# S5 parameters ahead of the input tiles, input weights split one tile ahead, and output matrices built for eight groups at a time

## The chip, the cores and the metric

The kernel runs on one core of one Trainium2 chip. The metric is the device time of one execution in microseconds (us). An engine is named by what it does: TensorE (PE: matmul, PEld: its weight load), VectorE (DVE), ScalarE (ACT), GpSimd (POOL) and SyncE (SP), whose queue issues nearly all transfers.

## What is computed

One layer of a hybrid diffusion backbone on 128 context tokens and 512 latent tokens (640 in all, 1024 channels): a token mixer with an S5 state-space branch and a pooling branch, and a squared-ReLU MLP, each with a modulated layer norm before and a gated residual after it. Cut to the part around the change:

```python
def s5_direction(u, s0, lam_re, lam_im, log_dt, b_re, b_im, c_re, c_im, d, reverse):
    dt = exp(log_dt)                       # 64 groups of 16 channels, 64 states each
    lam_bar = exp(lam * dt)
    b_bar = ((lam_bar - 1.0) / lam) * b_mat
    bu = einsum('blgh,gph->blgp', u, b_bar)
    _, s = associative_scan(a = lam_bar, bu, reverse)   # s[t] = lam_bar * s[t-1] + bu[t]
    return einsum('blgp,ghp->blgh', s, c_mat).real + d * u, s[last]

def token_mixer(h, s0_f, s0_b, grid_w, lp):
    z = h @ w_in + b_in                    # 3584 columns: u_a 1024, u_b 512, g_a 1024, g_b 1024
    y_f, y_b = s5_direction(u_a, ...), s5_direction(u_a, ..., reverse=True)
    v = gelu(y_f + y_b)
    v = v * sigmoid(v @ w_glu + b_glu)
    yb = pool_mix(u_b) @ w_proj_b
    return (sigmoid(g_a) * (v @ w_proj_a) + sigmoid(g_b) * yb) @ w_out + b_out
```

## The kernel before

All matrices are float32. A matmul with full precision is made of three passes over two halves (high, low) of both operands, so each weight tile is loaded (`wr`), its high half cast on ScalarE (L321) and its low half subtracted on VectorE (L322) by `wsplit`. One tile of the input projection (128 output channels, 640 tokens) is 48 matmuls of 320 columns at L336: eight steps over the input channels, three passes, two halves of the tokens. There are 28 such tiles: 0 to 7 give u of the S5 branch, 8 to 11 the pooling input, 12 to 27 the gates. `wr` has two buffers, `wh`, the split tile, three.

The S5 branch works on blocks of eight tokens. The 640 tokens are 80 blocks, and within a block the recurrence is done by matrices, between blocks by a scan of 63 steps of the state (`scan_step`, four VectorE operations each, L501 to L504; the first steps after step 0 do both sequences at once). The matrices are made in the kernel:

- `s5_angles` and `s5_params` (L104 to L210) turn `lam` and the time steps into powers of lam_bar: tables `pqt`, `pqs` for the output and `pwt`, `pws` for the input matrices. They are chains of short operations on VectorE with one Sin and a few copies on ScalarE.
- `gen_in(e)`, for four groups each and e from 0 to 15, makes the input matrix `wt`: it loads coefficients, forms a sum and a difference on GpSimd (L438, L439, in `coefs`), and calls `outer`, five VectorE operations of 512 elements (L424 to L431). Eight transposes on TensorE (L466) and copies on ScalarE give `w`. `in_proj(e)` then multiplies it by u, 32 small matmuls on `psz` (L480), and ScalarE writes the result into the states `zt` (L485). u comes back through DRAM in another layout, forward (`ud`) and with the blocks reversed by GpSimd (`urd`, L369, L370).
- `gen_q(e)` makes the output matrix `q` of four groups in the same way from `cpk`, and writes it to DRAM (`qd`). `gen_t(m)` multiplies the q of eight groups with the input matrices kept in `bm`, 64 small matmuls on `psq` (L533), and evacuates the result as `sq` by ScalarE (L538, L539) and VectorE (L540, L542). `psq` takes one of the two double PSUM banks that the tiles of the input projection take as well.

In program order: layer norm of the five token tiles `xs`; the first modulation; a loop over eight channel tiles that makes the normalised input `hx` and at once the input tiles 0 and 1, with `s5_angles` in the middle; `s5_params` after it; then a loop over tiles 2 to 7 with two `more_in` steps (each a `gen_in` and, one behind, an `in_proj`) after each tile, and `gen` (two `gen_q` and a `gen_t`) after tiles 5 and 7; five more `more_in`; then the scan with a `gen` in every ninth step, six in all, and one further input tile (`fill`, through `plain`) in every third step, sixteen in all. The last four tiles are computed in halves (`halves`, L606) among the steps of `out_proj`, after the scan.

Program order isn't the order on the engines. When the kernel is built, a planner walks through the program and queues, on each engine, the operation that comes first in the program among those whose inputs and buffers it expects to be ready. At run time each engine then works through its queue in order, and waits where an input is late. The number of buffers of a tile (`bufs`) thus also decides how early an operation can be queued. `q5` (the q of four groups) and `sq` have two buffers, `c3` (their coefficients) three, `b3` (coefficients of the input matrices) and `oy` (a scratch tile of `outer`) two and one.

Of the kernel before, what the change touches and what calls it, by code (L numbers as in the profile page):

```python
# [10 lines left out]
F32 = mybir.dt.float32  # L11
# [27 lines left out]
def hybrid_kernel(ctx: ExitStack, tc: tile.TileContext, xin, cc, w_ada0, w_ada, w_in, w_glu, w_pa, w_pool, w_pb,  # L39
# [263 lines left out]

    xs = []
# [4 lines left out]
    dma(lamt, lam)  # L309
# [45 lines left out]
    qd = dp.tile([16, P, 8 * P], F32, name="qd")  # L355
# [16 lines left out]

    hx = []
    hl0, hl1 = wsplit(w_in[0]), wsplit(w_in[1])
    wss += [shift_scale_load(q) for q in (1, 2, 3)]
    shift_scale(0)
    pu0, pu1 = bank2(), bank2()
    for k in range(KT):
# [11 lines left out]
        if k == 4:  # L390
            ang = s5_angles()
# [8 lines left out]
    s5_params(*ang)  # L400
# [13 lines left out]
    oyt = sub_tile("oy", 1, genp)  # L414

    def outer(o, tab, tsum, cf, e, sign):


        sh = [P, 4, TC, 16]
        tr, ti, ts = [t[:, 4 * e:4 * e + 4, :].unsqueeze(3).broadcast_to(sh) for t in (tab[:, 0], tab[:, 1], tsum)]  # L420
        c0, c1, c2 = [cf[:, :, f, :].unsqueeze(2).broadcast_to(sh) for f in (1, 3, 4)]
        o0, o1 = [o[:, :, r, :].rearrange("p l (s i) -> p l s i", i=16) for r in range(2)]
        y = oyt(sh, "oy")
# [8 lines left out]

    def coefs(tile_of, src, e, sign):

        c = tile_of([P, 4, 5, 16], "cf")
        dma(c[:, :, 1:3, :], src[:, e])
        E = nc.gpsimd
        E.tensor_tensor(c[:, :, 3, :], c[:, :, 1, :], c[:, :, 2, :], op=ALU.add)  # L438
        E.tensor_tensor(c[:, :, 4, :], c[:, :, 2 if sign > 0 else 1, :], c[:, :, 1 if sign > 0 else 2, :],  # L439
                        op=ALU.subtract)  # L440
        return c
# [13 lines left out]
    def gen_in(e):  # L455

        b3 = coefs(sub_tile("b3", 2), bpk, e, 1)
        wt = mat4([P, 4, 2, P], "wt")
        outer(wt, pwt, pws, b3, e, 1)
# [48 lines left out]
    c3t, qgt, sqt = sub_tile("c3", 3, genp), sub_tile("q5", 2, genp), sub_tile("sq", 2, genp)  # L508

    def gen_q(e):  # L510

        c3 = coefs(c3t, cpk, e, -1)
        S.mul(c3[:, :, 0, :], c3[:, :, 2, :], -1.0)
        q = qgt([P, 4, 2, 160], "q")
        S.copy(q[:, :, :, 0:16], c3[:, :, 1::-1, :])
        S.copy(q[:, :, :, 144:160], c3[:, :, 1::-1, :])
        outer(q[:, :, :, 16:144], pqt, pqs, c3, e, -1)
        dma(qd[e].rearrange("p (l r c) -> p l r c", l=4, r=2), q[:, :, :, 16:144])
        qs[e] = q

    def gen_t(m):
# [3 lines left out]
        for gq in range(2):  # L525
            e = 2 * m + gq
            q = qs.pop(e)
# [57 lines left out]
    def plain(m, func, dst):  # L585
        ps = mm(wsplit(w_in[m]), hx)
        g = gt([P, NT], "g")
        S.activation(tv(g), v2(ps), func, bias=colt[:, C_BIN + m:C_BIN + m + 1])
        dma(dst, g)
# [606 lines left out]
```

## Time and profile before

| | us |
|---|---|
| median of 3 runs | 1055.24 |
| lowest and highest run | 1054.97, 1055.71 |
| the profiled execution, its own time | 1057.73 |
| its span, first to last instruction | 1056.0 |

| engine | busy us | share of the span |
|---|---|---|
| TensorE matmul | 991.3 | 94% |
| TensorE weight load | 894.4 | 85% |
| VectorE | 691.6 | 65% |
| ScalarE | 403.0 | 38% |
| GpSimd | 110.9 | 11% |

The profile is one execution; times in it are counted from the start of its span. Matmuls are pipelined and their ends are modelled, so a stretch in which TensorE counts as busy can still hold less work than it could. A row of the timeline merges instructions of a kind that follow each other; its length is from the start of the first to the end of the last, and operations that follow each other overlap a little, so a spacing is read from start to start. What stands in brackets is the idle time of the engine before the row, and what ended it.

### The profile page before, as it was taken

To read this page: it belongs to the slowest core of one execution; us is meant where nothing else is said; L and a number is where in the kernel's file an instruction comes from. 1 tells how busy PE (TensorE), PEld (TensorE's weight loads), DVE (VectorE), ACT (ScalarE), POOL (GpSimd) and SP (SyncE) were. 2 spreads that over 40 slices of the span, in tenths; PEclk is the share of its full clock that TensorE was granted. 3 is DMA by queue.
4 is the path that set the end of the run, shared out by engine and by line. 5 is a ranking of instruction groups with operands and counts; after the bars stand their busy time and mean duration, and the time that the engine had idled before them with its cause. 6 is when DMAs were issued, how large, how long until landed. Compare 5 with 4: busy or idle time off the path is not lost.

```text
span 1056.0 us, 18416 instructions
## 1 busy us (share of the span) xinstructions
PE 991.3 (94%) x7464; PEld 894.4 (85%) x7464; DVE 691.6 (65%) x1203; ACT 403.0 (38%) x683; POOL 110.9 (11%) x164
## 2 busy tenths in 40 slices
PE   4998989998998899999999999989999999999997
PEld 2887878988897799998987898868998899889886
DVE  7698769998921334545847955498864586458686
ACT  5457454322212534422222544313661266116610
POOL 0243210310069000300000000000000000000000
PEclk9999899999999798999999999999999999999999
DMA  9566666855498587977752134513222222212421
GB/s 362 191 176 179 168 182 194 255 166 170 119 284 248 161 253 244 360 231 252 247 182 83 31 110 155 150 45 100 81 100 73 68 80 100 80 60 81 162 78 60
DMA packets 117373, 166.85 MB, mean 158 GB/s; under 512 B 48104, under 2 KB 80872, under 8 KB 117288
## 3 DMA queue, kind: packets, MB, share of 16 engines
q1 hardware_dynamic: 111912, 146.27, 43.9%
q0 software_dynamic: 5376, 19.40, 5.4%
q8 instruction: 59, 0.97, 0.4%
q14 instruction: 26, 0.21, 0.1%
HBM read 135.30 MB, written 30.34 MB: 157 GB/s over the span
## 4 chain that ended last, share of the span: by engine, by line
PE 61%; DVE 16%; DMA 10%; issue 6%; ACT 5%; SPq 2%; DVEq 0%; ACTq 0%; POOL 0%; POOLq 0%
PE ps L336 20%; PE ps L1073 13%; PE ps L1006 8%; PE psx L1006 6%; PE pse L1096 3%; PE ps L886 3%; DVE wh L322 2%; DMA cf<-in_cpk_dram 2%; DMA yd<-y 2%; DVE ta L501 1%; DVE zt L504 1%; PE psa L236 1%; PE psz L480 1%; DVE ta L503 1%; PE ps L1096 1%
## 5 line engine op out<-in xcount | busy, mean ns | idle before, releaser
L336 PE MATMUL ps<-hk,wh 128*128 128x320 f32 x1344 | 217.1, 318 | 10.0 <-DVE sq L542 5.1
L336 PEld LDWEIGHTS ps<-hk,wh 128*128 128x128 f32 x1344 | 202.0, 192 | 18.6 <-issue 6.0
L322 DVE TENSOR_TENSOR wh<-wr,wh 128x1024 fp32r<-128x1024 f32 (+1 forms) x113 | 128.5, 1138 | 101.8 <-ACT wh L321 100.7
L321 ACT CAST wh<-wr 128x1024 fp32r<-128x1024 f32 (+1 forms) x113 | 109.3, 967 | 164.7 <-PE ps L1073 87.6
L1073 PE MATMUL ps<-wh,fx 128*128 128x512 f32 x720 | 166.1, 392 | 5.2 <-DVE x L852 3.0
L1073 PEld LDWEIGHTS ps<-wh,fx 128*128 128x128 f32 x720 | 135.7, 189 | 34.2 <-DVE x L852 3.4
L336 PEld LDWEIGHTS ps<-gx,wh 128*128 128x128 f32 x384 | 56.4, 187 | 3.3 <-issue 2.9
L336 PE MATMUL ps<-gx,wh 128*128 128x320 f32 x384 | 58.7, 310 | 0.0
L336 PEld LDWEIGHTS ps<-vx,wh 128*128 128x128 f32 x384 | 56.4, 188 | 2.5 <-ACT sg L813 2.1
L336 PE MATMUL ps<-vx,wh 128*128 128x320 f32 x384 | 58.1, 311 | 0.0
L224 POOL DMA_DIRECT2D wa<-in_w_ada_dram x32 | 16.9, 534 | 300.8 <-PE psa L236 110.2
L1006 PE MATMUL psx<-h,wh 128*128 128x320 f32 x288 | 47.5, 308 | 0.0
L1006 PE MATMUL ps<-h,w 128*128 128x320 f32 x288 | 46.5, 307 | 0.0
L438 POOL TENSOR_TENSOR cf<-cf 128x64 f32<-128x64 f32 x32 | 24.8, 776 | 191.0 <-DMA cf<-in_cpk_dram 95.7
L1006 PEld LDWEIGHTS psx<-h,wh 128*128 128x128 f32 x288 | 43.7, 187 | 0.2
L1006 PEld LDWEIGHTS ps<-h,w 128*128 128x128 f32 x288 | 43.2, 187 | 0.0
L573 PE MATMUL psy<-zt,q 64*128 64x80 f32 x512 | 42.1, 276 | 0.6 <-issue 0.6
L851 DVE TENSOR_TENSOR ps<-ps,gate 128x512 f32<-128x512 f32 (+2 forms) x39 | 28.1, 749 | 19.2 <-PE ps L1073 14.2
L573 PEld LDWEIGHTS psy<-zt,q 64*128 64x128 f32 x512 | 35.3, 190 | 4.2 <-issue 4.2
L886 PE MATMUL ps<-wo,mx 128*128 128x512 f32 x150 | 36.6, 392 | 0.7 <-ACT wo L321 0.7
L336 PE MATMUL ps<-ybx,wh 128*128 128x320 f32 x192 | 32.6, 328 | 2.7 <-ACT wh L321 2.7
L886 PEld LDWEIGHTS ps<-wo,mx 128*128 128x128 f32 x150 | 27.9, 188 | 7.2 <-ACT wo L321 1.5
(263 smaller groups left out, 1656.9 us busy)
## 6 DMA issues: line engine op xcount, KB each, us to landing
wr<-in_w_m_dram SPq DMA_DIRECT2D x64, 512.0 KB
wa<-in_w_ada_dram POOLq DMA_DIRECT2D x32, 512.0 KB, 5.0
wr<-in_w_in_dram SPq DMA_DIRECT2D x28, 512.0 KB
qd<-q SPq DMA_DIRECT2D x16, 512.0 KB
q<-qd SPq DMA_DIRECT2D x16, 512.0 KB
x<-in_xin_dram SPq DMA_DIRECT2D x10, 512.0 KB
wa<-in_w_ada_dram SPq DMA_DIRECT2D x10, 512.0 KB
tm<-sd SPq DMA_DIRECT2D x8, 512.0 KB
```

The source lines that it names most:

```text
L224: nc.gpsimd.dma_start(w, w_ada[self.mod, :, k * D:(k + 1) * D])
L236: T.matmul(self.ps[32 * q:32 * q + 32, 0:256], sc[:, k, :], w[:, q * 256:(q + 1) * 256], start=(k == 0), stop=(k == KT - 1), skip_group_ch ...
L321: S.copy(hi, raw)
L322: V.tensor_tensor(lo, raw, hi.bitcast(F32), op=ALU.subtract)
L336: T.matmul(ps[:, n, 0:ln], hl[:, wh, k * P:(k + 1) * P], xk[:, xh, o:o + ln], start=(k == 0 and i == 0), stop=(k == nk - 1 and i == 2))
L438: E.tensor_tensor(c[:, :, 3, :], c[:, :, 1, :], c[:, :, 2, :], op=ALU.add)
L573: T.matmul(o, q[d, l, i, :], zt[d, 0:NC // 2, i, 4 * e + l, :], start=(i == 0), stop=False, skip_group_check=True)
L851: V.tensor_tensor(ps, ps, g[:, c0:c1], op=ALU.mult)
L886: T.matmul(ps[:, n, :], mx[k][:, xh, t * P:(t + 1) * P], wo[k][:, wh, n * 512:(n + 1) * 512], start=(k == 0 and i == 0), stop=(k == KT - 1 ...
L1006: T.matmul(ps, hl[:, wh, c + k * P:c + (k + 1) * P], rq[b][:, xh, k, :], start=(start and k == 0 and i == 0), stop=(stop and k == 3 and i ...
L1073: T.matmul(pt[t], fx[k][:, xh, t * P:(t + 1) * P], hl[:, wh, kk * 512:(kk + 1) * 512], start=(k == 0 and i == 0), stop=(k == 7 and i == 2))
L1096: T.matmul(ps[n][:, 0:ln], fx[k][:, xh, t * P:(t + 1) * P], hl[:, wh, o_:o_ + ln], start=(k == 0 and i == 0), stop=(k == 7 and i == 2))
```

## The change

`lam` is loaded ahead of the five token tiles. `s5_angles` and `s5_params` are called one after the other ahead of the loop over the channel tiles. `next_w` hands out the split weights of the input tiles in the order in which they are used and splits one more than is asked for. `gen_q` makes q for eight groups in operations of 1024 elements; `q5` and `sq` have one buffer, `c3` two, `b3` three. Coefficients are formed in place: three columns where there were five. `gen_q(0)` stands ahead of the loop over tiles 2 to 7, and each further `gen_q` behind the `gen_t` of the eight groups before; `gen_t(0)` and `gen_t(1)` come after tiles 4 and 6, `gen_t(2)` and `gen_q(3)` before the last three `more_in`. One `fill` stands before the scan; in the scan are five `gen_t` and four `gen_q`, eleven steps apart, and fifteen `fill`, in every fourth step. The work of the input projection, of `gen_in` and of the output stage is the same; the scratch of q in DRAM has rows twice as long.

```diff
@@ -301,12 +301,12 @@
             V.scalar_tensor_tensor(modc[:, mod, 2 * q:2 * q + 2, :], src[:, mod, :, 0:2], float(mod), b,
                                    op0=ALU.add, op1=ALU.add)
+    dma(lamt, lam)
     xs = []
     for t in range(NTT):
         x = mat4([P, D], "x")
         xs.append(x)
         dma(x, xin[t])
-    dma(lamt, lam)
     dma(ident, cst)
     dma(colt, cols)
     wss = [shift_scale_load(0)]
@@ -352,7 +352,7 @@
     urd = dp.tile([KT, TC, P, NC], F32, name="urd")
     yd = dp.tile([KT, TC, P // 8, 8 * NC], F32, name="yd")
     sd = dp.tile([KT, 32, 4, 480], F32, name="sd")
-    qd = dp.tile([16, P, 8 * P], F32, name="qd")
+    qd = dp.tile([KT, P, 16 * P], F32, name="qd")
     mbd = dp.tile([KT, P, NT], F32, name="mbd")
     gad = dp.tile([KT, P, NT], F32, name="gad")
     gbd = dp.tile([KT, P, NT], F32, name="gbd")
@@ -370,10 +370,19 @@
         nc.gpsimd.tensor_copy(ur[:, :, CP:NC], uj[:, :, NC - 1:CP - 1:-1])
         dma(urd[m].rearrange("j p c -> p j c"), ur)
+    order_w, ready_w = [*range(2, 12), *range(20, 28), *range(12, 20)], []
+    def next_w():
+        while order_w and len(ready_w) < 2:
+            ready_w.append(wsplit(w_in[order_w.pop(0)]))
+        return ready_w.pop(0)
     hx = []
     hl0, hl1 = wsplit(w_in[0]), wsplit(w_in[1])
     wss += [shift_scale_load(q) for q in (1, 2, 3)]
     shift_scale(0)
+    s5_params(*s5_angles())
     pu0, pu1 = bank2(), bank2()
     for k in range(KT):
         pa, pb = bank("pst"), bank("pst")
@@ -387,8 +396,6 @@
         V.tensor_copy(hk[:, 0, :], hf)
         V.tensor_tensor(hk[:, 1, :], hf, hk[:, 0, :].bitcast(F32), op=ALU.subtract)
         hx.append(hk)
-        if k == 4:
-            ang = s5_angles()
         if k % 2:
             if k < KT - 1:
                 shift_scale(k // 2 + 1)
@@ -397,7 +404,6 @@
                     mm_k(pu, hl, hx[kk], kk, KT, SEG)
     ua_evac(0, pu0)
     ua_evac(1, pu1)
-    s5_params(*ang)
     dma(dd, ddg)
     V.tensor_tensor(dd[:, 0, :], dd[:, 0, :], dd[:, 1, :], op=ALU.add)
@@ -411,16 +417,17 @@
     dma(s0t, s0)
-    oyt = sub_tile("oy", 1, genp)
-    def outer(o, tab, tsum, cf, e, sign):
-        sh = [P, 4, TC, 16]
-        tr, ti, ts = [t[:, 4 * e:4 * e + 4, :].unsqueeze(3).broadcast_to(sh) for t in (tab[:, 0], tab[:, 1], tsum)]
-        c0, c1, c2 = [cf[:, :, f, :].unsqueeze(2).broadcast_to(sh) for f in (1, 3, 4)]
+    oyt, bt = sub_tile("oy", 1, genp), sub_tile("b3", 3)
+    c3t, qgt, sqt = sub_tile("c3", 2, genp), sub_tile("q5", 1, genp), sub_tile("sq", 1, genp)
+    def outer(o, tab, tsum, cf, g0, n, sign):
+        sh = [P, n, TC, 16]
+        tr, ti, ts = [t[:, g0:g0 + n, :].unsqueeze(3).broadcast_to(sh) for t in (tab[:, 0], tab[:, 1], tsum)]
+        c0, c1, c2 = [c.unsqueeze(2).broadcast_to(sh) for c in cf]
         o0, o1 = [o[:, :, r, :].rearrange("p l (s i) -> p l s i", i=16) for r in range(2)]
-        y = oyt(sh, "oy")
+        y = oyt([P, 8, TC, 16], "oy")[:, 0:n]
         V.tensor_tensor(y, ts, c0, op=ALU.mult)
         V.tensor_tensor(o0, ti, c1, op=ALU.mult)
         V.tensor_tensor(o1, tr, c2, op=ALU.mult)
@@ -430,16 +437,6 @@
         else:
             V.tensor_tensor(o1, o1, y, op=ALU.subtract)
-    def coefs(tile_of, src, e, sign):
-        c = tile_of([P, 4, 5, 16], "cf")
-        dma(c[:, :, 1:3, :], src[:, e])
-        E = nc.gpsimd
-        E.tensor_tensor(c[:, :, 3, :], c[:, :, 1, :], c[:, :, 2, :], op=ALU.add)
-        E.tensor_tensor(c[:, :, 4, :], c[:, :, 2 if sign > 0 else 1, :], c[:, :, 1 if sign > 0 else 2, :],
-                        op=ALU.subtract)
-        return c
     bmv = bm[:, 0:G * 32].rearrange("p (g b i) -> p g b i", g=G, b=2)
     us = {}
@@ -454,9 +451,12 @@
     def gen_in(e):
-        b3 = coefs(sub_tile("b3", 2), bpk, e, 1)
+        b = bt([P, 4, 3, 16], "b")
+        dma(b[:, :, 0:2, :], bpk[:, e])
+        nc.gpsimd.tensor_tensor(b[:, :, 2, :], b[:, :, 0, :], b[:, :, 1, :], op=ALU.add)
+        nc.gpsimd.tensor_tensor(b[:, :, 1, :], b[:, :, 1, :], b[:, :, 0, :], op=ALU.subtract)
         wt = mat4([P, 4, 2, P], "wt")
-        outer(wt, pwt, pws, b3, e, 1)
+        outer(wt, pwt, pws, [b[:, :, i, :] for i in (0, 2, 1)], 4 * e, 4, 1)
         S.copy(bmv[0:64, 4 * e:4 * e + 4, :, :], wt[0:64, :, :, 0:16])
         S.copy(bmv[64:128, 4 * e:4 * e + 4, :, :], wt[64:128, :, :, P - 16:P])
         w = mat4([P, 4, 2, P], "w")
@@ -505,26 +505,27 @@
     qs, outs, tms = {}, {}, {}
-    c3t, qgt, sqt = sub_tile("c3", 3, genp), sub_tile("q5", 2, genp), sub_tile("sq", 2, genp)
-    def gen_q(e):
-        c3 = coefs(c3t, cpk, e, -1)
-        S.mul(c3[:, :, 0, :], c3[:, :, 2, :], -1.0)
-        q = qgt([P, 4, 2, 160], "q")
-        S.copy(q[:, :, :, 0:16], c3[:, :, 1::-1, :])
-        S.copy(q[:, :, :, 144:160], c3[:, :, 1::-1, :])
-        outer(q[:, :, :, 16:144], pqt, pqs, c3, e, -1)
-        dma(qd[e].rearrange("p (l r c) -> p l r c", l=4, r=2), q[:, :, :, 16:144])
-        qs[e] = q
+    def gen_q(m):
+        c = c3t([P, 8, 3, 16], "c")
+        dma(c[:, :, 0:2, :].rearrange("p (a l) r i -> p a l r i", a=2), cpk[:, 2 * m:2 * m + 2])
+        nc.gpsimd.tensor_tensor(c[:, :, 2, :], c[:, :, 0, :], c[:, :, 1, :], op=ALU.add)
+        q = qgt([P, 8, 2, 160], "q")
+        for o in (0, 144):
+            S.copy(q[:, :, 0, o:o + 16], c[:, :, 0, :])
+            S.mul(q[:, :, 1, o:o + 16], c[:, :, 1, :], -1.0)
+        nc.gpsimd.tensor_tensor(c[:, :, 1, :], c[:, :, 0, :], c[:, :, 1, :], op=ALU.subtract)
+        outer(q[:, :, :, 16:144], pqt, pqs, [c[:, :, i, :] for i in (0, 2, 1)], 8 * m, 8, -1)
+        dma(qd[m].rearrange("p (l r c) -> p l r c", l=8, r=2), q[:, :, :, 16:144])
+        qs[m] = q
     def gen_t(m):
         ps2 = bank2("psq")
         pss = [ps2[:, 0], ps2[:, 1]]
         for gq in range(2):
-            e = 2 * m + gq
-            q = qs.pop(e)
+            e, q = 2 * m + gq, qs[m][:, 4 * gq:4 * gq + 4]
             for r in range(2):
                 c0 = 4 * e * 32 + r * 16
                 for fb in range(2):
@@ -551,7 +552,7 @@
             dma(tm.rearrange("p l a f -> p (l a) f"), src)
             tms[m] = tm
         q = qt([P, 4, 2, P], "q")
-        dma(q.rearrange("p l r c -> p (l r c)"), qd[e])
+        dma(q.rearrange("p l r c -> p (l r c)"), qd[m][:, (e % 2) * 1024:(e % 2) * 1024 + 1024])
         u = ut([P, 4, NC], "u")
         for hf, d in enumerate((ud, urd)):
             dma(u[64 * hf:64 * hf + 64], d[m, 4 * hf:4 * hf + 4].rearrange("j (i g) c -> (j i) g c", g=8)
@@ -583,7 +584,7 @@
     def plain(m, func, dst):
-        ps = mm(wsplit(w_in[m]), hx)
+        ps = mm(next_w(), hx)
         g = gt([P, NT], "g")
         S.activation(tv(g), v2(ps), func, bias=colt[:, C_BIN + m:C_BIN + m + 1])
         dma(dst, g)
@@ -596,7 +597,7 @@
         while fillers:
             m, func, dst = fillers.pop(0)
-            hl, ps = wsplit(w_in[m]), bank2()
+            hl, ps = next_w(), bank2()
             for k in range(KT):
                 mm_k(ps, hl, hx[k], k, KT, SEG)
                 if k == 3:
@@ -624,17 +625,18 @@
     nin = [0]
-    def gen(m):
-        gen_q(2 * m)
-        gen_q(2 * m + 1)
-        gen_t(m)
+    gen_q(0)
     for m in range(2, 8):
-        ua_evac(m, mm(wsplit(w_in[m]), hx))
+        ua_evac(m, mm(next_w(), hx))
         more_in(2, 1)
-        if m in (5, 7):
-            gen((m - 5) // 2)
-    more_in(5)
+        if m in (4, 6):
+            gen_t(m // 2 - 2)
+            gen_q(m // 2 - 1)
+    more_in(2)
+    fill(1)
+    gen_t(2)
+    gen_q(3)
+    more_in(3)
     prectx.close()
     sub[0] = s5ctx.enter_context(tc.tile_pool(name="post", bufs=1, reuse_waits="tile"))
     qt, tmt = sub_tile("q", 4), sub_tile("tm", 3)
@@ -708,9 +710,11 @@
             S.copy(last, state(CP))
             dma(nstate, last)
             S.copy(state(CP), s0t)
-        if s % 9 == 5 and s // 9 < 6:
-            gen(2 + s // 9)
-        if s % 3 == 0 and s < 48:
+        if s % 11 == 3 and s < 50:
+            gen_t(3 + s // 11)
+            if s < 40:
+                gen_q(4 + s // 11)
+        if s % 4 == 0 and s < 60:
             fill(1)
     genctx.close()
     mixctx = ctx.enter_context(ExitStack())
```

## Rows read from the trace of the kernel before

**Rows 1.** stretches: start:end, length; PE, PEld, DVE, ACT, POOL busy; clock, DMA, GB/s

```profile
0.00:52.60 52.60, 36.11 (x396) 29.18 (x396) 35.19 (x123) 25.97 (x47) 6.30 (x18) 1.00 0.75 277
67.10:92.00 24.90, 21.31 (x232) 18.47 (x233) 22.37 (x32) 18.04 (x43) 8.92 (x14) 1.00 0.74 199
103.10:113.60 10.50, 7.00 (x71) 5.03 (x72) 8.72 (x13) 3.15 (x9) 1.68 (x4) 0.67 0.85 224
135.90:144.80 8.90, 5.61 (x75) 4.28 (x74) 8.56 (x13) 2.78 (x9) 0.76 (x2) 0.81 0.79 220
158.00:166.00 8.00, 5.43 (x73) 4.71 (x73) 6.91 (x11) 5.73 (x17) 1.92 (x4) 0.79 0.19 50
52.60:170.00 117.40, 104.37 (x1120) 92.62 (x1120) 92.28 (x147) 69.15 (x171) 33.34 (x59) 0.94 0.63 168
170.00:291.00 121.00, 112.64 (x1092) 108.80 (x1091) 112.35 (x318) 33.78 (x70) 14.17 (x16) 1.00 0.63 190
```

**Rows 2.** groups of TensorE's matmuls, 52.6 to 170 us: busy, mean ns, idle before

```profile
L336 PE MATMUL ps<-hk,wh 128*128 128x320 f32 x352 | 60.6, 323 | 0.0
L480 PE MATMUL psz<-u,w 128*64 128x80 f32 x512 | 28.3, 254 | 0.0
L466 PE MATMUL pst<-ident,wt 128*128 128x128 f32 x128 | 19.7, 286 | 6.2 <-DVE wt L427 6.2
L533 PE MATMUL psq<-q,bm 64*32 64x128 f32 x128 | 3.6, 310 | 6.8 <-DVE q L427 6.8
```

**Rows 3.** the same groups in the scan stage, 170 to 291 us

```profile
L336 PE MATMUL ps<-hk,wh 128*128 128x320 f32 x707 | 106.7, 310 | 7.8 <-DVE sq L542 5.1 <-ACT g L588 2.7
L533 PE MATMUL psq<-q,bm 64*32 64x128 f32 x384 | 6.9, 274 | 0.0
```

**Rows 4.** timeline of TensorE around the first matrix step: start, length, operation, idle before

```profile
99.75 1.03 PE L466 MATMUL pst<-ident,wt 128*128 128x128 f32 x8
100.72 1.33 PE L480 MATMUL psz<-u,w 128*64 128x80 f32 x32
101.97 1.09 PE L466 MATMUL pst<-ident,wt 128*128 128x128 f32 x8
106.60 0.66 PE L533 MATMUL psq<-q,bm 64*32 64x128 f32 x16 [3.53 <-DVE q L427]
```

**Rows 5.** timeline of SyncE's queue, ScalarE and VectorE: the S5 parameters and their surroundings

```profile
3.56 0.49 SPq L309 DMA_DIRECT2D big<-in_lam_dram  x1
...
29.04 0.27 ACT L295 COPY row<-psa 128x128 f32<-128x128 f32 x1 [5.87 <-PE psa L292]
...
65.02 0.89 DVE L209 TENSOR_TENSOR pws<-pwt 128x512 f32<-128x512 f32 x1 [0.37 <-ACT pwt L208]
```

**Rows 6.** timeline of VectorE: the split of the input tile before that step

```profile
103.51 1.23 DVE L322 TENSOR_TENSOR wh<-wr,wh 128x1024 fp32r<-128x1024 f32 x1 [2.91 <-ACT wh L321]
```

**Rows 7.** timeline of VectorE, then its group of L431 from 170 to 291 us

```profile
126.18 0.68 DVE L426 TENSOR_TENSOR wt<-pwt,cf 128x512 f32<-128x512 f32 x1
126.78 0.68 DVE L427 TENSOR_TENSOR wt<-oy,wt 128x512 f32<-128x512 f32 x1
...
272.61 1.22 DVE L322 TENSOR_TENSOR wh<-wr,wh 128x1024 fp32r<-128x1024 f32 x1
273.75 0.28 DVE L503 TENSOR_TENSOR ta<-ta,zt 128x128 f32<-128x128 f32 x1
...
L431 DVE TENSOR_TENSOR q<-q,oy 128x512 f32<-128x512 f32 x10 | 6.9, 691 | 0.0
```

**Rows 8.** waits from 170 to 291 us: total, times, longest

```profile
ACT cf L513 <- DMA cf<-in_cpk_dram: 44.7, 5, 15.2
...
POOL ub L654 <- PE psq L533: 26.7, 1, 26.7
```

**Rows 9.** timeline of GpSimd: the same copy twice

```profile
60.81 4.00 POOL L369 COPY ujr<-uj 128x128 f32<-128x128 f32 x1 [5.46 <-ACT uj L364]
...
133.74 0.29 POOL L369 COPY ujr<-uj 128x128 f32<-128x128 f32 x1 [3.30 <-ACT uj L364]
```

## The prediction

> **What bounds the kernel now.** I read the busy times of the engines stretch by stretch first, because one average over the span (TensorE 94% busy) hides four stages with different limits [rows 1]. Up to 52.6 us the layer norm, the first modulation and the first two input tiles run; from 52.6 to 170 the input projection of the S5 branch with the generation of its matrices; from 170 to 291 the serial scan on VectorE with sixteen gate tiles ("fillers") on TensorE beside it; from 291 to 412 the output projection. What follows is nearly solid matmul and isn't touched. A busy TensorE isn't a working one, so next I priced its work in the two middle stages by its groups [rows 2, 3]. In the scan 707 matmuls of 320 columns take 106.7 us, 0.151 each, and 64 of the small matmuls on psq take 6.9 / 6 = 1.15. From the timeline eight transposes take 0.97 (99.75 to 100.72) and 32 matmuls of the state input 1.25 (100.72 to 101.97) [rows 4]. By these prices the second stage holds 352 x 0.151 + 512 x 0.039 + 128 x 0.121 + 2 x 1.15 = 91.0 us of work in 117.4 us: 26.4 are lost. The scan stage holds 106.7 + 6.9 = 113.6 in 121: 7.4 lost, beside a VectorE busy 112.35; both engines are near their limit there. So the second stage is the place.
>
> Then the waits say where the 26.4 lie. The matrix step L533 waits 6.8 us in two pieces for q and the transposes L466 wait 6.2 for wt, both VectorE's outer products [rows 2]. Around the first L533, 103.1 to 113.6, the 71 matmuls (by the timeline 32 on psq, 7 on ps, 32 on psz: 2.9 us by the prices; the kinds of the next stretches are counted in the same way) take 10.5: 7.6 lost, more than the wait of 3.53 itself, because the granted clock of that stretch is 0.67, that is, it fell to the 1.2 GHz level after the idle time [rows 1, 4]. Around the second, 135.9 to 144.8, 8.9 us hold 3.1: 5.8 lost, clock 0.81. From 158 to 166, 8.0 hold 3.5: 4.5 lost. From 67.1 to 92, where the S5 matrices have only just begun, 24.9 hold 57 x 0.151 + 48 x 0.121 + 128 x 0.039 = 19.4: 5.5 lost. These four are 23.4 of the 26.4; 3.0 are scattered.
>
> **Part A, S5 parameters first (to 52.6 us).** The load of lam goes ahead of five x loads on SyncE's queue. Its issue is 0.49 [rows 5], so each x, and the first layer norm, starts up to 0.49 later. What it serves: today the last of the parameters on VectorE, the sum L209, starts at 65.02 and ends at 65.9, and no wt can be built before that [rows 5]. Moved up, at most 65.9 - 52.6 = 13.3 us of VectorE work go ahead of 52.6, with q of the first eight groups (5.7, below). VectorE is busy 35.19 of these 52.6, so 17.4 are free [rows 1]: 13.3 + 5.7 - 17.4 = 1.6 don't fit. I take 1.6 + 0.49 = +2.1. Lower end +0.5, the issue alone, if the other work slides behind 52.6 without harm. Upper end: all 13.3 are queued ahead of the first hk and cover only the 5.87 us in which ScalarE waits for the modulation matmuls [rows 5]: +7.4. The steps on ScalarE (a Sin with its table load, eight copies) lie in the same gap; if the Sin falls between two square roots, two more table loads come, and I leave them to this end too.
>
> **Part B, the second stage.** Its work afterwards: 6 x 48 matmuls for u, one filler of 48, the same 512 and 128, and three psq steps: 336 x 0.151 + 20.0 + 15.5 + 3.45 = 89.7. The losses, one by one. (1) The two stalls on q, 13.4: gen_q now stands one step ahead of the gen_t that reads it (q of groups 0 to 7 before the loop, the next right behind each gen_t), and the weight tile of the next input matmul is split one tile ahead, so TensorE has both at hand. I take them at 0; upper end 13.4. Both are needed: at 103 us TensorE had no split weight either, since the cast on ScalarE came last (L322 at 103.51, 2.91 us idle on VectorE) [rows 6]. (2) The start, 5.5: the wt of the first groups no longer wait for L209; the u that come back through DRAM still are as late as now, so I take 2.5. (3) The tail, 4.5: VectorE waits behind coefficient loads; fewer and larger ones now, 3.0. (4) The scattered 3.0 stay. (5) New waits. VectorE gets four double q here (22.8 us, below) for six single ones; the trace can't show how the new order meshes, and I put 5.0 there: four waits of the size of a transposing wait, 6.2 / 5 [rows 2]. Lost: 13.5, so 103.2 us against 117.4: -14.2. Ends: the loss rate of the scan stage (7.4 in 121) would leave 89.7 + 5.9 = 95.6, -21.8; the old 26.4 would leave 116.1, -1.3.
>
> The double operations: one outer product is five operations of 512 elements at a spacing of 0.60 (126.18 to 126.78), 3.0 us; one of 1024 elements spaces 1.14 (272.61 to 273.75), so five are 5.7 for two, 0.3 saved a pair, 2.4 in all [rows 7]. Half the issues of q and of its coefficients also leave SyncE's queue; nothing on the path waits for those issues alone, so 0 for that.
>
> **Part C, the scan.** TensorE: 15 fillers and five gen_t, 720 x 0.151 + 5 x 1.15 = 114.5. VectorE: ten outer products go (one operation of each is the row of L431, x10), 30.0, and four double ones come, 22.8: 112.35 - 7.2 = 105.2 [rows 1, 7]. So TensorE bounds it, plus its waits: 7.8 now, 5.1 for the last step of sq (psq shares two PSUM pairs with the fillers) and 2.7 for g on ScalarE [rows 3]. The latter stands behind L513, which waits 44.7 us in five pieces for coefficients [rows 8]; with two slots for one load in each period they can come a period early: 0. Of the 5.1 I keep 4.0. 118.5 against 121: -2.5. Ends: no wait -6.5, the old waits +1.3.
>
> At the same place a rule speaks against longer operations. The row first: GpSimd's copy L369 of 128 elements takes 0.29 alone, and 4.00 while VectorE runs without a pause, six of its operations long [rows 9]. The Trainium skill, "SBUF — State Buffer", section "Who interferes with whom", says that a VectorE operation with two SBUF inputs and a GpSimd operation that reads SBUF take the port as an exclusive lock for a whole instruction. By it an operation of 1.14 in place of 0.60 holds a u copy 0.54 longer, and if all eight copies were on the path the sum would be 4 us higher; by the row GpSimd waits for a pause, not for the end of one operation, and the length costs 0. That row decides for the sum.
>
> **Part D, the output stage.** Unchanged work; q is read from rows twice as long in DRAM, in pieces of the same size: 0. GpSimd's pooling there starts only once the last psq is done (a wait of 26.7 [rows 8]); the last gen_t moves from step 50 to 47 of the scan, which may start it some steps earlier: lower end -5, upper end +3 if its reads of SBUF fall into the scan.
>
> **Sum.** The profiled execution took 1057.73 us (span 1056.0), 2.49 above the median of 1055.24. 1057.73 + 2.1 - 14.2 - 2.5 = 1043.1; less 2.49, **1041** for the median.
>
> **Rivals.** First, **the waits only change their name**: VectorE's outer products and the way of u through DRAM pace the second stage whatever the order. For it: wt is a wait already [rows 2], and VectorE is busy 92.28 of 117.4 there [rows 1]. Against: TensorE stalls at the same moments as VectorE, on work that could have been done before. Half of B left gives 1048; the low end of B gives 1055.24 + 2.1 - 1.3 - 2.5 = 1054. Second, **slower: the single q buffer**. It was two tiles of four groups, now it is one of eight, so gen_q(m+1) can't write before the 64 matmuls of gen_t(m) are done and q has been written to DRAM. VectorE runs in order: behind the waiting operation stand the scan steps and the splits, and behind these TensorE. A gen_t can stand behind one filler, 48 x 0.151 = 7.2, so the wait is up to 7.2 + 1.15 = 8.4 for each of seven gen_q; half of it, seven times, is +29: 1070. It decides from (1057.4 - 1041) / 7 = 2.3 us each. Against: operations are queued by when the planner expects their inputs, and VectorE's waits in the scan are small today [rows 3, 6]. Third, **more than forecast**: B at the loss rate of the scan, 1041 - 7.6 = 1033, and with pooling earlier 1028.
>
> **How the numbers follow.** Forecast, 1034 to 1048: 0.48. Better, 1026 to 1034: 0.13. Between 1048 and 1053.1: 0.10. Within 0.2% (1053.1 to 1057.4, what a measurement can tell from no change): 0.10. Slower, by the q buffer or the upper end of A with no gain in B: 0.19. Faster is 0.71. The range leaves out some 0.05 below 1027 and 0.15 above 1058.
>
> **What would show it.** Right: no idle time of L533 for q, the granted clock at 1.00 between 100 and 145, the first wt before 60 us, the scan's first steps near 158, and a scan stage of about 118. Wrong: an L425 or L424 on VectorE waiting for psq or for q's write (the second rival); L466 or L480 waiting longer than now (the first); the loop over the channel tiles ending several us after 52.6 (A's upper end).

## The result, and the profile after

The changed kernel takes **1065.28 us** (median of 4 runs, 1062.74 to 1067.66), where the kernel before takes 1055.47 (4 runs): a ratio of 1.0088, interval 1.0059 to 1.0117. It is 0.9% slower, and outside the forecast's range. Its profiled execution has a span of 1062.9 us, 6.9 more than before.

First the stretches of the changed kernel, in the columns of [rows 1]: two that stand in [rows 1] as well, and then the four stages at their own bounds.

```profile
0.00:52.60 52.60, 31.79 (x372) 26.72 (x372) 44.97 (x141) 28.97 (x49) 7.74 (x20) 1.00 0.76 273
52.60:170.00 117.40, 110.32 (x1304) 99.91 (x1304) 86.59 (x116) 65.41 (x166) 30.73 (x49) 0.99 0.70 196
...
0.00:60.10 60.10, 37.61 (x399) 32.12 (x399) 51.08 (x150) 30.52 (x52) 7.94 (x20) 0.97 0.76 266
60.10:171.60 111.50, 104.56 (x1279) 94.53 (x1278) 81.60 (x108) 65.45 (x166) 30.53 (x48) 1.00 0.70 194
171.60:278.80 107.20, 104.59 (x928) 102.08 (x928) 102.68 (x270) 29.70 (x55) 22.13 (x20) 1.00 0.67 200
278.80:300.70 21.90, 0.03 (x1) 0.02 (x1) 21.59 (x23) 1.84 (x2) 21.53 (x23) 0.55 0.27 85
```

Up to 52.6 us VectorE has 45.0 us of work instead of 35.2 and TensorE falls behind (31.8 instead of 36.1). In the second stage TensorE does 184 more instructions in the same 117.4 us (128 of them the small ones on psq), at a clock of 0.99 instead of 0.94. And there is a stretch that before didn't have: 21.9 us in which TensorE does nothing, while VectorE and GpSimd are both busy throughout, with 23 instructions each. The timeline of TensorE shows the bounds of the stages:

```profile
60.14 3.05 PE L336 MATMUL ps<-hk,wh 128*128 128x320 f32 x19
...
142.10 0.53 PE L480 MATMUL psz<-u,w 128*64 128x80 f32 x4 [2.34 <-DMA u<-ud]
...
171.57 10.67 PE L336 MATMUL ps<-hk,wh 128*128 128x320 f32 x71 [1.55 <-ACT g L589]
...
300.71 1.15 PE L574 MATMUL psy<-zt,q 64*128 64x80 f32 x8 [21.88 <-POOL us L667]
```

TensorE's timeline of the kernel before, at the same points:

```profile
176.13 21.39 PE L336 MATMUL ps<-hk,wh 128*128 128x320 f32 x144
...
289.28 1.16 PE L533 MATMUL psq<-q,bm 64*32 64x128 f32 x64
291.00 0.68 PE L573 MATMUL psy<-zt,q 64*128 64x80 f32 x8 [0.56 <-issue]
```

The channel-tile loop ends at 60.14, where tile 2 begins (before: 52.6). At 171.57 there are 672 matmuls of input tiles left ahead of the output stage; the kernel before comes to that point at 176.13, with one matrix step fewer done. The output stage begins at 300.71 (before: 291.00). So the 6.9 us are made of these four:

| stage, us | before | after | difference |
|---|---|---|---|
| to the end of the channel-tile loop | 52.6 | 60.1 | +7.5 |
| to 672 matmuls left | 123.5 | 111.4 | -12.1 |
| to the first matmul of the output stage | 114.9 | 129.1 | +14.3 |
| the rest | 765.0 | 762.2 | -2.8 |

The groups of TensorE, 52.6 to 170 us, which answer to [rows 2]; the kernel before's stall for q at L533 is gone from the group that takes its place, L534:

```profile
L336 PE MATMUL ps<-hk,wh 128*128 128x320 f32 x408 | 67.7, 320 | 2.5 <-DVE hk L396 2.0 <-DVE hk L397 0.5
L480 PE MATMUL psz<-u,w 128*64 128x80 f32 x512 | 24.6, 237 | 3.5 <-DMA u<-ud 3.5
L466 PE MATMUL pst<-ident,wt 128*128 128x128 f32 x128 | 19.1, 279 | 1.9 <-DVE wt L434 1.7
L534 PE MATMUL psq<-q,bm 64*32 64x128 f32 x256 | 6.6, 276 | 0.0
```

In the scan, 170 to 301 us, the same view shows 4.2 us of TensorE's ordinary waits (7.8 in [rows 3]):

```profile
L336 PE MATMUL ps<-hk,wh 128*128 128x320 f32 x672 | 100.6, 310 | 4.2 <-ACT g L589 2.5 <-DVE sq L543 1.7
```

What costs the time is the last piece of the third stage. GpSimd's timeline there (its spans are rough):

```profile
256.42 0.75 POOL L656 MEMSET ub<- 128x784 f32 x1 [16.20 <-PE psq L534]
...
271.22 0.55 POOL L660 DMA_DIRECT2D ic<-in_invc_dram  x1 [11.21 <-DVE ta L503]
...
273.21 1.50 POOL L667 TENSOR_TENSOR us<-ub 128x783 f32<-128x783 f32 x1
...
275.35 2.08 POOL L671 TENSOR_TENSOR ic<-us,ic 128x128 f32<-128x128 f32 x2
...
291.97 3.06 POOL L667 TENSOR_TENSOR us<-us 128x781 f32<-128x781 f32 x2
295.11 1.72 POOL L671 TENSOR_TENSOR ic<-us,ic 128x128 f32<-128x128 f32 x2
296.79 1.77 POOL L672 TENSOR_TENSOR ic<-ic,ub 128x128 f32<-128x128 f32 x2
```

and VectorE's timeline, a step of the scan just ahead of it and some rows beside it:

```profile
270.43 0.28 DVE L502 TENSOR_TENSOR tb<-lmi,zt 128x128 f32<-128x128 f32 x1
...
272.22 3.58 DVE L322 TENSOR_TENSOR wh<-wr,wh 128x1024 fp32r<-128x1024 f32 x1
...
276.20 1.37 DVE L502 TENSOR_TENSOR tb<-lmi,zt 128x128 f32<-128x128 f32 x1
...
282.89 2.00 DVE L501 TENSOR_TENSOR ta<-lmr,zt 128x128 f32<-128x128 f32 x1
...
290.81 2.82 DVE L503 TENSOR_TENSOR ta<-ta,zt 128x128 f32<-128x128 f32 x1
293.66 1.51 DVE L504 TENSOR_TENSOR zt<-ta,tb 128x128 f32<-128x128 f32 x1
...
299.03 1.57 DVE L504 TENSOR_TENSOR zt<-ta,tb 128x128 f32<-128x128 f32 x1
```

The pooling branch (`pool_mix`) begins here at 256.4, where its first memset ends a wait for the psq matmuls of the last `gen_t`, which run at 255.2 (before: at 289.3). GpSimd then waits another 11.21 us, until 271.2, before its next load; from 273.2 on its additions run while the scan is still at work. Each takes 1.5 us or a little more. An operation of the scan that takes 0.28 alone takes up to 2.82 beside them, the split at L322 3.58 instead of 1.22. From 272.22 to the end of the last L504 at 300.6 there are six scan steps and two splits. Undisturbed, a step is 1.06 from start to start and the two splits are 1.14 and 0.60, 8.1 in all; here they last 28.4. That is +20.3, and the rest of the stage gained 6.0.

### The profile page after: what moved, and what is told of

It reads as the page before. It is cut to its first block, busy times and chain, and to the rows that moved or that the text cites. A ratio compares the mean times of both kernels' runs of the same rounds, so it can differ in the third digit from the quotient of the medians.

```text
span 1062.9 us, 18300 instructions
## 1 busy us (share of the span) xinstructions
PE 986.3 (93%) x7464; PEld 894.0 (84%) x7464; DVE 706.7 (66%) x1163; ACT 400.4 (38%) x667; POOL 108.1 (10%) x148
## 4 chain that ended last, share of the span: by engine, by line
PE 60%; DVE 14%; DMA 12%; issue 6%; ACT 4%; POOL 3%; SPq 1%; DVEq 0%; ACTq 0%; POOLq 0%
PE ps L336 20%; PE ps L1077 13%; PE ps L1010 8%; PE psx L1010 6%; PE pse L1100 3%; PE ps L890 2%; PE psy L574 2%; DMA wr<-in_w_in_dram 2%; DVE wh L322 2%; DMA wa<-in_w_ada_dram 1%; PE psa L236 1%; PE psz L480 1%; DMA wr<-in_w_out_dram 1%; PE ps L1100 1%; DVE zt L504 1%
## 5 line engine op out<-in xcount | busy, mean ns | idle before, releaser
L336 PE MATMUL ps<-hk,wh 128*128 128x320 f32 x1344 | 214.6, 317 | 9.5 <-DVE hk L396 4.4
L322 DVE TENSOR_TENSOR wh<-wr,wh 128x1024 fp32r<-128x1024 f32 (+1 forms) x113 | 130.1, 1152 | 105.9 <-ACT wh L321 104.9
L574 PE MATMUL psy<-zt,q 64*128 64x80 f32 x512 | 43.9, 285 | 21.9 <-POOL us L667 21.9
L589 ACT ACTIVATE g<-ps,colt 128x640 f32<-128x640 f32 x16 | 12.7, 795 | 65.5 <-PE ps L336 65.5
```

Source lines behind the costliest of these rows:

```text
L322: V.tensor_tensor(lo, raw, hi.bitcast(F32), op=ALU.subtract)
L336: T.matmul(ps[:, n, 0:ln], hl[:, wh, k * P:(k + 1) * P], xk[:, xh, o:o + ln], start=(k == 0 and i == 0), stop=(k == nk - 1 and i == 2))
L574: T.matmul(o, q[d, l, i, :], zt[d, 0:NC // 2, i, 4 * e + l, :], start=(i == 0), stop=False, skip_group_check=True)
```

## The experiments

The kernel before had medians from 1055.5 to 1061.8 on the chips of these runs, so each kernel is compared by its ratio to the runs of the kernel before on its own chip; a difference of two medians from different chips can be off by some us.

**Pooling held until the scan is over.** In each of the four poolings one operation makes the first element of the input depend on the last state:

```diff
         E.memset(u, 0.0)
+        z = state(NC - 1)[:, 0, 0:1]
+        E.tensor_tensor(u[:, 0:1], z, z, op=ALU.subtract)
```

> The changed kernel with one edit: each pooling starts with a difference of the scan's last state, written into a column that is zero anyway, so GpSimd can't pool before the scan has ended. Theory (pooling in the scan's last steps slows VectorE: six steps and two splits take 28.8 us, 271.9 to 300.7, in place of some 8): the scan ends near 281 us, the idle time of TensorE before the output stage (21.9 us) falls under 4, and the median is 1045 to 1050. Rival (VectorE's own order delays those steps, GpSimd only fills the time): the scan still ends near 300 and the median stays at 1065 or rises, since the pooling then ends later too.

1043.7 us, ratio 0.9842 (0.9807 to 0.9877), span 1042.2: a little better than the theory said, and its rival is out. VectorE's groups from 270 to 283 us are back at their length, and TensorE's output stage begins at 280.03, in its timeline:

```profile
L322 DVE TENSOR_TENSOR wh<-wr,wh 128x1024 fp32r<-128x1024 f32 x2 | 2.4, 1222 | 1.7 <-ACT wh L321 1.7
L502 DVE TENSOR_TENSOR tb<-lmi,zt 128x128 f32<-128x128 f32 x8 | 2.3, 284 | 0.0
```

```profile
280.03 0.68 PE L574 MATMUL psy<-zt,q 64*128 64x80 f32 x8 [1.40 <-issue]
```

By the spans the hold is worth 20.7 us, by the starts of the output stage (300.71, 280.03) the same; by the ratios (0.9842 against 1.0088) it is 2.5%, some 26 us. Nothing is lost behind: from there to the end both kernels take 762.2. Pooling's later start costs nothing.

**Pooling's arithmetic left out**, its memsets and loads kept:

```diff
-            n = pool3([P, 784], "us")
...
-            E.tensor_tensor(n[:, a:b_], s[:, a - d0:b_ - d0], s[:, a + d1:b_ + d1], op=ALU.add)
+            n = s
...
-            E.tensor_tensor(iv, sv, iv, op=ALU.mult)
-            E.tensor_tensor(iv, iv, uv, op=ALU.subtract)
```

> The changed kernel with GpSimd's arithmetic of the pooling left out (its sums, products and differences; fills and loads stay). Theory: VectorE's operations from 272 us on have their old lengths (0.2 to 0.3 us for a step's operation, 1.2 for a split) and the scan ends near 280 us; 1040 to 1048. Rival: the steps stay spread out to 300 us without GpSimd's arithmetic, 1060 or more.

1044.78 us, ratio 0.9854 (0.9805 to 0.9903), as the theory said. The memsets and transfers run at the old early place, and the scan beside them is undisturbed. GpSimd's timeline, then VectorE's group of 255 to 281 us:

```profile
274.07 1.43 POOL L658 DMA_DIRECT2D ub<-ubd  x2
275.49 0.77 POOL L656 MEMSET ub<- 128x784 f32 x1
```

```profile
L502 DVE TENSOR_TENSOR tb<-lmi,zt 128x128 f32<-128x128 f32 x21 | 6.0, 284 | 0.0
```

So it is the additions and products, not pooling's memory, loads or issues.

**Pooling held on an earlier state**, four steps ahead of the last (`state(NC - 5)` in the first edit):

> The changed kernel with pooling held on the state four scan steps before the last one instead of on the last. Theory (each scan step beside pooling lasts some 3 us longer): the last four steps and what follows them stretch, TensorE's wait ahead of the output stage grows from 1.4 to 8 to 15 us, and the time is 1048 to 1057. Rival (the 20 us of the changed kernel are the cost of pooling's start, its memory or its loads, and not of each step beside it): 1042 to 1046, as when it is held on the last state.

1059.37 us, ratio 0.9998 (0.9972 to 1.0024), span 1053.5. VectorE's and TensorE's timelines:

```profile
276.12 2.00 DVE L504 TENSOR_TENSOR zt<-ta,tb 128x128 f32<-128x128 f32 x1
278.15 0.59 DVE L501 TENSOR_TENSOR ta<-lmr,zt 128x128 f32<-128x128 f32 x1
278.67 1.77 DVE L502 TENSOR_TENSOR tb<-lmi,zt 128x128 f32<-128x128 f32 x1
280.36 1.76 DVE L503 TENSOR_TENSOR ta<-ta,zt 128x128 f32<-128x128 f32 x1
282.15 1.46 DVE L504 TENSOR_TENSOR zt<-ta,tb 128x128 f32<-128x128 f32 x1
```

Scan operations that last 1 to 2 us begin with the first addition, and TensorE's wait ahead of the output stage is 12.6 us where the hold on the last state has 1.4. The time is a little above the theory's upper end; its rival is out. With six steps beside pooling the output stage begins at 300.7, with four at 291.4, with none at 280.0: the cost goes with the steps that meet it, 2.8 us each with four and 3.4 with six, or 2.9 without the 3.4 us by which the two splits among the six are longer. The trace is of the fastest of ten executions (1055.63); by the ratios (0.9998 against 0.9842) the four steps cost 1.6%, some 16 us, so 2.8 is a low figure.

**The same collision made in the kernel before.** Its matrix steps in the scan are put seven steps apart instead of nine and nothing else is changed:

```diff
-        if s % 9 == 5 and s // 9 < 6:
-            gen(2 + s // 9)
+        if s % 7 == 3 and s // 7 < 6:
+            gen(2 + s // 7)
```

> The kernel before with one edit: the output matrices of a group are made at every seventh scan step instead of every eighth plus its offset, so the last of the six is done some ten steps of the scan earlier and GpSimd's pooling may begin while the scan still runs, as it does in the changed kernel. Nothing else of the change is in it. Theory (pooling beside the scan stretches the scan's short two-input VectorE operations): pooling's first pieces stand ahead of the scan's end in the trace, the VectorE operations of the steps beside it last 1.5 to 3 us where they last 0.3 to 1.2 elsewhere, TensorE has an idle stretch of more than 10 us ahead of the output stage, and the time is 1065 to 1080 where the kernel before has 1055 to 1060. Rival (the stretch in the changed kernel comes from its larger output matrices or its split, not from pooling as such): within 3 us of the kernel before. If pooling's inputs land only after the scan's end, the run says nothing on either.

1065.01 us, ratio 1.0059 (1.0034 to 1.0085): nearly as slow as the whole change, by moving the matrix steps of the scan and nothing else. GpSimd's, VectorE's and TensorE's timelines:

```profile
284.64 1.51 POOL L665 TENSOR_TENSOR us<-ub 128x783 f32<-128x783 f32 x1
...
286.78 1.71 POOL L669 TENSOR_TENSOR ic<-us,ic 128x128 f32<-128x128 f32 x2
288.45 1.71 POOL L670 TENSOR_TENSOR ic<-ic,ub 128x128 f32<-128x128 f32 x2
```

```profile
283.68 3.03 DVE L322 TENSOR_TENSOR wh<-wr,wh 128x512 fp32r<-128x512 f32 x1
286.63 3.68 DVE L504 TENSOR_TENSOR zt<-ta,tb 128x128 f32<-128x128 f32 x1
290.35 1.46 DVE L501 TENSOR_TENSOR ta<-lmr,zt 128x128 f32<-128x128 f32 x1
```

```profile
300.10 1.14 PE L573 MATMUL psy<-zt,q 64*128 64x80 f32 x8 [9.91 <-POOL ub L654]
```

The time is at the theory's lower end and the idle stretch, 9.91, just under the 10 that it named. The mechanism needs neither the double operations nor the single q buffer nor the parameters first; it needs the last `gen_t` early. **Eight steps apart** (`s % 8 == 4`) was too mild to test it:

> The kernel before with one edit: its six matrix steps in the scan come in every eighth step in place of every ninth, the last at step 44 in place of 50, so that the memory of the matrices, on which GpSimd's pooling waits, comes free before the scan has ended. Nothing else of the change is in it. Theory (early pooling slows the scan's last steps): pooling starts 6 us or more before the scan's end, the operations of the steps beside it take 0.5 to 2 us each, and the kernel gets slower by 5 to 15 us. Rival (the slow tail belongs to the new order of the q and split operations): within 3 us of the kernel before.

1056.99 us, ratio 0.9995 (0.9971 to 1.0019). Pooling's memset came at 282.81, but GpSimd then waited 12.17 us for another transfer, until 298.6, and the first addition came at 300.6, after the scan's end; nothing met. Inconclusive.

**S5 parameters put back** (angles at the fifth channel tile, the rest behind the loop; the load of `lam` stays first), once in the changed kernel and once in the held one:

```diff
-    s5_params(*s5_angles())
...
+        if k == 4:
+            ang = s5_angles()
...
+    s5_params(*ang)
```

> The changed kernel with the two S5 calls put back (angles at the fifth channel tile, parameters behind the loop); all else as changed. Theory (S5 ahead of the channel tiles costs 7.5 us there, since VectorE is full until 58 us): the loop ends near 52 us again, the second stage starts some 7 us earlier but its input matrices come later; if these don't matter the median is 1058, and if the start of the second stage loses its old 5 us it stays within 2 us of 1065. Rival (the early parameters are what shortened the second stage): 1068 or more.

> Both edits at once: pooling held until the scan has ended, and the S5 calls put back. Theory with independent parts: the two gains add, 1038 to 1045 against 1055 of the kernel before. Rival (an earlier second stage only fills the scan with work that is late anyway): the same as the hold alone, within 2 us.

1073.04 us, ratio 1.0125 (1.007 to 1.018), and 1050.45, ratio 0.9908 (0.9876 to 0.994). The held one is 7 us slower than with the parameters first, so both its theory (1038 to 1045) and its rival (no change) were wrong. The unheld one has its rival's time (1068 or more), but its interval overlaps the changed kernel's 1.0088 (1.0059 to 1.0117). In the held one the loop ends at 51.9, 8.2 us earlier, and yet the point with 672 matmuls left comes at 176.76, 5.7 later. Its TensorE timeline shows where both are lost:

```profile
69.55 0.44 PE L468 MATMUL pst<-ident,wt 128*128 128x128 f32 x2 [2.78 <-DVE wt L436]
...
115.38 0.70 PE L482 MATMUL psz<-u,w 128*64 128x80 f32 x4 [4.73 <-DMA u<-ud]
...
176.76 5.54 PE L336 MATMUL ps<-hk,wh 128*128 128x320 f32 x36 [1.55 <-ACT g L591]
```

Neither kernel waits for q at its matrix step, though the parameters are late here, and with the parameters first alone (below) the stall stays: that leaves `gen_q`, made one step ahead and in its new form, as what removes it. This wasn't run by itself.

**Only the angles first**, the rest of the parameters behind the loop, in the held kernel:

```diff
-    s5_params(*s5_angles())
+    ang = s5_angles()
...
+    s5_params(*ang)
```

> The changed kernel with pooling held until the last state of the scan is there, and with the second half of S5's parameters put back behind the loop over channel tiles, while the angles stay ahead of it. Theory A (the 7.5 us by which the channel tiles end late are VectorE's time for the parameters, and the half that is put back needn't be early): the loop ends 3 to 5 us earlier and the time is 1038 to 1042. Theory B (the scan's first output matrix has to be ready when the filler stage begins, and the parameters are on its chain): the loop ends earlier, the stage behind it begins later, and the time is 1046 to 1052, as with both halves put back (1050).

1050.94 us, ratio 0.9918 (0.9891 to 0.9945): the loop ends at 56.2, 3.9 earlier than in the held kernel, but the 672-left point comes at 179.64 and a wait of 5.93 for u at 118.4 has come. The time is theory B's.

**S5 first alone, in the kernel before** (`lam` first, both calls ahead of the loop, nothing else):

> The kernel before with the S5 part alone: lam loaded first, angles and parameters ahead of the channel tiles. Theory after the last runs (the early parameters delay the channel tiles by some 7 us and give back more than that in the second stage): the loop ends near 58 us in place of 52.6, the second stage ends 0 to 8 us earlier than before, 1047 to 1056 against 1055 (where the scan ends before pooling starts). Rival (it only pays together with the earlier q): the 7 us at the start stay, 1060 or more.

1058.01 us, ratio 1.0002 (0.9979 to 1.0025): neither faster nor slower, at the upper end of the theory by the ratio and between theory and rival by the median. The loop ends at 57.4, the 672-left point comes 3.1 us earlier than before, and both stalls for q are still there, 3.29 and 3.28:

```profile
105.70 0.45 PE L531 MATMUL psq<-q,bm 64*32 64x128 f32 x16 [3.29 <-DVE q L425]
```

**No split ahead**, and **the first q two tiles later**, both in the held kernel:

```diff
-        while order_w and len(ready_w) < 2:
+        while order_w and len(ready_w) < 1:
```

> The changed kernel with pooling held until the scan's end, and without the split one tile ahead: each input tile is split when it is asked for. Theory (the stalls on q and on the split weight were one thing, and both parts are needed): the second stage loses 3 to 8 us again, 1047 to 1052. Rival (the planner splits early enough by itself): within 2 us of the kernel with the hold alone, 1043.7.

```diff
-    gen_q(0)
...
+        if m == 2:
+            gen_q(0)
```

> The changed kernel with pooling held until the scan's end, and the first q made behind input tile 2 in place of ahead of it. Theory (part of the 7.5 us at the start is the five operations of 1.1 to 1.3 us of the first q between the hk of the channel tiles): the loop over the channel tiles ends 3 to 5 us earlier and the median is 1039 to 1042. Rival (the time at the start is set by the S5 chain ahead of the first hk, or is given back later): within 1.5 us of 1043.7.

1041.66 us, ratio 0.9855 (0.9829 to 0.9881), and 1044.66, ratio 0.9872 (0.9834 to 0.9911): neither can be told from the held kernel's 0.9842. Both theories missed; the rivals hold, the first by its ratio and the second by its time. Without the split ahead there is no stall for q either, and the 672-left point comes at 170.99 (171.04 with it). With q later the loop ends at 57.5 instead of 60.1, with no gain at the end.

**The changed kernel again**, on the chip on which the versions held four steps early and with only the angles first ran:

> The changed kernel itself, unedited, beside the other three on the same chip, so that the held version and it are compared on one chip. Theory: 1060 to 1068, and 18 to 24 us above the held versions. Rival (the chips differ by as much as the hold is worth): under 1052.

1066.68 us, ratio 1.0073 (1.005 to 1.0096), output stage at 297.8 behind a wait of 18.52. The chips aren't the cause. It is 7.3 and 15.7 us above those two versions, less than the 18 to 24 that were expected; the plain held kernel wasn't run on this chip, and by the ratios (0.9842, 1.0073) lies 2.3% below.

## Why the prediction was wrong

**The step that failed is Part D's upper end.** It named pooling "some steps earlier", put "+3 if its reads of SBUF fall into the scan", and took 0. The place and the trigger were right: the last `gen_t` frees the memory that pooling waits for ([rows 8], 26.7 us before, 16.20 after, the memset now at 256.4). The size wasn't: +20.3 us in the trace. I gave it no price per step. Nor was there a gain for the lower end to take: with pooling held, the rest takes the same 762.2. [Rows 9] show an operation on one of the two engines held up while the other runs, 4.00 instead of 0.29; I read from them what GpSimd loses, and never asked what VectorE loses when GpSimd runs without a pause. And each piece of pooling is 1.5 us, five times a scan operation. Six steps of 1.06 among such pieces can't be a matter of 3 us. With +20 in place of 0 the sum would have been 1061.

**The rule was weighed at the wrong place.** The trace has it first: a scan operation with two inputs in SBUF lasts 0.28 alone, 0.28 beside GpSimd's memsets and DMA issues where no arithmetic is near (256 to 260 us, and throughout the run without arithmetic), and up to 2.82 beside GpSimd's additions, whose own median there is 1.52 (1.50 in the held kernel). The Trainium skill, "SBUF — State Buffer", section "Who interferes with whom", says that a VectorE instruction with two SBUF inputs contends with a GpSimd instruction that reads SBUF, not with one that only writes it. The trace agrees with that. How long an operation is held up is another matter: L504 at 286.63 in the kernel before with early matrix steps took 3.68, past the end of all four multiplications and subtractions beside it on GpSimd (286.78 to 290.16), so it lost more than one turn. I had used the rule only to ask whether longer q operations hold a copy on GpSimd, where nothing came of it: the longest of the eight copies L369 now takes 0.76.

**Part A** came out at its upper end: +7.5, where I took +2.1 and named +7.4 as the end. That the end fits so well is luck: it had all the parameters ahead of the first hk, and here the first two hk, at 27.4 and 29.6, come among them, while q adds its part. The extra table loads that were left to this end didn't come: the first 70 us have three in either kernel. The sum of free time was the wrong measure: VectorE's 17.4 free us didn't lie where the parameters could use them. The parameters' rows stand ahead of and between those of hk, and the last of them, L209, ends at 38.6; q's five double operations stand among the later hk:

```profile
37.92 0.69 DVE L209 TENSOR_TENSOR pws<-pwt 128x512 f32<-128x512 f32 x1 [2.24 <-ACT pwt L208]
...
47.39 0.48 DVE L396 CAST hk<-hf 128x640 fp32r<-128x640 f32 x1
...
48.72 1.22 DVE L434 TENSOR_TENSOR q<-oy,q 128x1024 f32<-128x1024 f32 x1
49.85 1.22 DVE L438 TENSOR_TENSOR q<-q,oy 128x1024 f32<-128x1024 f32 x1
...
55.01 0.48 DVE L396 CAST hk<-hf 128x640 fp32r<-128x640 f32 x1
```

Taking the second half of the parameters out ends the loop 3.9 earlier, taking q out 2.6. But the loop's end isn't what sets the time: neither edit gains at the end; with the parameters late, wt and u are waited for instead.

**Part B** was near. The forecast's B ends with 720 matmuls and five matrix steps left, the table's stage with 672 and four. At the table's bounds B is 103.2 + 48 x 0.151 + 1.15 = 111.6, -11.9; the table has -12.1. The stalls on q are gone, as taken, and the clock is 1.00 from 60.1 on. "Both are needed", q earlier and a weight split ahead, was wrong: without the split ahead the stage is as short. The split that came last in [rows 6] was late together with q, and I took that for a second cause; what delayed it there these runs don't settle. At the start of the stage the three waits for wt (1.27, 1.12 and 1.00 us at 68.4, 78.5 and 90.8 in the kernel before) are gone. The new wait is u through DRAM, 3.5 in the group L480, where I took 5.0; of the 6.2 for wt at L466 1.9 are left. VectorE made three double q there, at 100, 128 and 158 us, not four: I counted the first in A as well as in B, which changes no term of the sum.

**Part C** without pooling gained somewhat more than I said. The held kernel goes from 171.04 to 280.03, 109.0 against 114.9: -5.9, of which about 1.15 is the matrix step that it had done earlier. At these bounds my C is 118.5 - 7.25 - 1.15 = 110.1, -4.8. TensorE's waits there, which I took as 4.0 for sq and 0 for g, are 2.0 and 2.5.

**The sum.** With pooling held the change gives 1043.7, the forecast's 1041 within 3 us (by its ratio, 0.9842 x 1055.24 = 1038.6), but out of terms that miss in both directions: +7.5, -12.6, -5.9 and -2.8 against +2.1, -11.9, -4.8 and 0 (by the spans, -13.8 against -14.6). Most of A's miss of 5.4 is made up by the others, more than half of that by the -2.8 after the start of the output stage, which no term foresaw. That stretch takes 761 to 767 us in the fourteen traces, so the -2.8 isn't shown to come from the change. The near agreement is partly luck.

**The rivals.** "Waits only change their name" isn't borne out: by the forecast's prices the stage from the end of the loop to 672 matmuls left holds 98.1 us of work in 111.4, 13.3 lost, where the kernel before had 96.9 in 123.5, 26.6 lost. The single q buffer, priced at +29, isn't seen: no wait of VectorE for psq or for q's write shows in the scan of the changed kernel, and the held kernel has the single buffer and is 1.6% faster than before. It put the chance of "slower" on the wrong mechanism.

**The version to keep** is the changed kernel with pooling held: 1.6% below the kernel before (0.9842), and by the ratios 2.3 to 2.5% below the changed one (20.7 us by the spans).

## What to carry to other kernels

When work moves earlier, ask what it frees, who waits for that, and beside what the released work will then run: here an engine off the path, set free 34 us early, cost one and a half times what all the edits had gained (20.7 against 13.8 us). A chain of short VectorE operations with two inputs in SBUF, on the critical path, should have no GpSimd arithmetic beside it; one cheap operation that makes GpSimd wait for the end of the chain gave all of it back. And price a possible collision per operation that meets it, not as one sum.

## What the runs showed of the hardware

GpSimd was hardly slowed by the collision and VectorE was: pooling's four additions of 783 elements have a median of 1.516 us (longest 1.936) in the changed kernel, where they meet the scan, 1.496 (longest 1.503) in the held kernel, while VectorE's operations of 128 x 128 go from 0.28 to as much as 3.68. In [rows 9] it was the other way round: a short copy on GpSimd took 4.00 us, and it ended at 64.81, in the pause of 0.37 us that VectorE made ahead of its row at 65.02 [rows 5]. What decides which of the two goes on isn't shown. Beside the additions some operations that begin during a DMA issue are long too (L503 at 290.81, 2.82); GpSimd's spans are rough, and without its arithmetic none is. In TensorE's pause of 21.9 us the granted clock fell to 0.55, near its 1.2 GHz level. And the time of a stage didn't follow its start: in the held kernel three edits that ended the first loop 2.6, 3.9 and 8.2 us earlier made it no faster, and the last two made it some 7 us slower.
